# Row products of an encoder block: moving columns and banks downwards in every second set of eight pieces, high parts at eight starts

## The chip, the cores and the metric

The kernel runs on one core of a Trainium2 chip. The metric is the device time of one execution in microseconds (us); lower is better. "Before" is the kernel without the change, "after" the one with it.

## The reference

One layer of a streaming encoder on 256 tokens of 2048 features, all in float32: a half-weighted SwiGLU feed-forward, a mixing block, cross-attention to 256 memory tokens, a second feed-forward and a last norm.

```python
x = x + 0.5 * swiglu(rms_norm(x, ffn1_norm), ffn1_w_up, ffn1_w_down)
h = rms_norm(x, mix_norm)
proj = h @ w_in                       # q, f, i, g, x-branch, gelu gate, two branch gates
...                                   # HGRN2 gives y_a, RG-LRU gives y_b
g = sigmoid(gates + b_gate)
merged = g[0] * (y_a @ w_branch_a) + g[1] * (y_b @ w_branch_b)
x = x + merged @ w_out
x = x + cross_attention(rms_norm(x, xattn_norm), rms_norm(mem, mem_norm), wq, wkv, wo)
x = x + 0.5 * swiglu(rms_norm(x, ffn2_norm), ffn2_w_up, ffn2_w_down)
return rms_norm(x, final_norm)
```

## The kernel before, in words

All weight matrices are streamed once from memory, in pieces of 128 partitions x 2048 columns of float32 (1 MB). A piece lands in a tile `raw` (three buffers). ScalarE writes its high part `h` (rounded to the matmul type float32r, line 126), VectorE the low part `l = raw - h` (line 127); each has three buffers of its own. Activations are held the same way, as a high and a low half. A product of two such numbers is three matmuls: high by high, low by high, high by low.

The pieces come in the order of a list, `plan`, and `weights()` prepares each two ahead of its use. A tile is taken from its pool in turn, and the writer of a buffer waits for the matmuls that last read it. Beyond that the order of the work on each engine is that of the program's text.

Between the two feed-forwards there are two ways to multiply. In `product` (lines 246 and 250; `in`, `q`, `k`) slices of the weight piece are the stationary operand and the activations move. In `rows_product` (lines 267, 268 and 270; `v`, `gate`, `ab`, `out`, `mv`, `o`) the activations are stationary, 128 tokens at a time, and the weight piece moves, 512 columns in one matmul. A piece holds four such slices (`j`, four steps of the contraction) for two halves of the tokens (`t`), so it takes 4 x 2 x 3 = 24 matmuls, each with a weight load of its own: 16 that read `h` and 8 that read `l`. Two PSUM banks, one for each half of the tokens, gather two to four pieces, and are then read by VectorE or ScalarE. The numbers of pieces are `v` 8, `gate` 32, `ab` 16, `out` 16, `mv` 16 and `o` 16.

The feed-forwards take their up-projection apart in a scheme with fewer products (lines 465, 466 and 468), with the weights moving in the same shapes; their tiles `h` come from the same pool.

Of the kernel before, what the change touches and what calls it, by code (L numbers as in the profile page):

```python
# [9 lines left out]
F32R = mybir.dt.float32r  # L10
# [3 lines left out]
P = 128  # L14
# [53 lines left out]
def block_kernel(ctx: ExitStack, tc: tile.TileContext, xT, xin, memT, vec, gfin, bgate, lruw, wu1, wd1, win, wv,  # L68
# [4 lines left out]
    def pool(name, bufs, **kw):  # L73
        return ctx.enter_context(tc.tile_pool(name=name, bufs=bufs, **kw))
# [3 lines left out]
    hp = pool("h", 3)  # L78
    lp = pool("l", 3)
# [19 lines left out]
    def bank(name="acc"):  # L99
        return psum.tile([P, 512], F32, name=name, tag="acc")  # L100
# [24 lines left out]
    def split(h, l, raw):  # L125
        done["high"] = act.activation(h, raw, ACT.Copy).ins  # L126
        done["low"] = dve.tensor_tensor(out=l, in0=raw, in1=h.bitcast(F32), op=ALU.subtract).ins  # L127

    def split_tiles():
        return hp.tile([P, 2048], F32R, name="h", tag="h"), lp.tile([P, 2048], F32R, name="l", tag="l")  # L130


    plan, ahead = [], []
# [12 lines left out]
    def plan_columns(name, w, which):  # L146
        plan.extend(((name, i), w[i], "plain") for i in which)

    def plan_rows(name, w, g):
        plan.extend(((name, g, kq), w[g, kq], "plain") for kq in range(w.shape[1]))  # L150

    plan_ffn("ffn1", wu1, wd1)
    for hf in range(2):
        for base in (8, 0):
            plan_columns("in", win, range(base + hf * 4, base + hf * 4 + 4))
        plan_rows("v", wv, hf)
        plan_columns("in", win, range(16 + hf * 4, 20 + hf * 4))
# [3 lines left out]
    for name, w, n in (("gate", wg, 8), ("ab", wab, 8), ("out", wout, 4)):  # L161
        for g in range(n):
            plan_rows(name, w, g)
    plan_columns("q", wq, range(KT))
    plan_columns("k", wk, range(KT))
    for name, w in (("mv", wvm), ("o", wo)):
        for g in range(4):
            plan_rows(name, w, g)
# [6 lines left out]
    def weights(*key):  # L175
        while plan and len(ahead) < 2:
            i = next(planned)
            k, src, kind = plan.pop(0)
            if i == 0:
                in_turn.enter_context(tc.manual_schedule(engines={sp.engine, act.engine, dve.engine}))  # L180
            if i < len(head):
                head[i]()
            if plan and plan[0][2] == "added":
                begun.append(begin_added(plan[0][1]))
            ahead.append((k, prepare(src, kind, 4 if i < 4 else 1)))
            if i in rest:
                rest[i]()
            if i == 7:
                in_turn.close()
        k, w = ahead.pop(0)  # L190
        assert k == key, (k, key)
        return w
# [3 lines left out]
    def begin_added(src):  # L196

        raw = rawp.tile([P, 2048], F32, name="raw", tag="raw")
        l = lp.tile([P, 2048], F32R, name="l", tag="l")
        sp.dma_start(raw, src)  # L200
        act.activation(l, raw, ACT.Copy, scale=-1.0)
        nc.gpsimd.dma_start(l, src, accum_op=ALU.add)
        return raw, l

    def prepare(src, kind, cuts=1):

        if kind == "added":
            raw, l = begun.pop(0)
            h = hp.tile([P, 2048], F32R, name="h", tag="h")
            done["high"] = act.activation(h, raw, ACT.Copy).ins  # L210
            return h, l
        raw = rawp.tile([P, 2048], F32, name="raw", tag="raw")
        n = 2048 // cuts
        if kind == "plain":
            h, l = split_tiles()
            for a in range(0, 2048, n):
                sp.dma_start(raw[:, a:a + n], src[:, a:a + n])
                split(h[:, a:a + n], l[:, a:a + n], raw[:, a:a + n])
            return h, l
        sp.dma_start(raw, src)  # L220
        td = scoped["wide"].tile([P, 2048], F32, name="td", tag="wide")
        two = [v[:, a:a + 1024].rearrange("p (i n) -> p i n", i=2) for v, a in ((td, 0), (raw, 512))]
        dve.tensor_tensor(out=two[0], in0=raw[:, None, :512].broadcast_to([P, 2, 512]), in1=two[1], op=ALU.subtract)  # L223
        dve.tensor_tensor(out=td[:, 1024:1536], in0=raw[:, 1024:1536], in1=td[:, :512], op=ALU.subtract)
        dve.tensor_tensor(out=td[:, 1536:], in0=raw[:, 1536:], in1=td[:, 1024:1536], op=ALU.subtract)
        h, l = split_tiles()
        if kind == "fast":
            split(h[:, 512:], l[:, 512:], raw[:, 512:])
        else:
            act.activation(l[:, 512:], raw[:, 512:], ACT.Copy, scale=-1.0)  # L230
            nc.gpsimd.dma_start(l[:, 512:], src[:, 512:], accum_op=ALU.add)
            done["high"] = act.activation(h[:, 512:], raw[:, 512:], ACT.Copy).ins
        th = hp.tile([P, 2048], F32R, name="h", tag="h")
        tl = scoped["wide"].tile([P, 2048], F32R, name="tl", tag="wide")
        for a in (0, 1024):
            split(th[:, a:a + 1024], tl[:, a:a + 1024], td[:, a:a + 1024])
        return (h, l), (th, tl)
# [21 lines left out]
        low(range(KT - 4 if was_late else 0, KT))  # L259
        return acc  # L260

    def rows_product(accs, xs, w, k0, first, last):

        terms = [(xs[k0 + j], t, j) for j in range(4) for t in range(2)]
        h, l = ([v[:, j * 512:(j + 1) * 512] for j in range(4)] for v in w)
        for x, t, j in terms:
            pe.matmul(accs[t], x[:, t * P:][:, :P], h[j], start=first and j == 0, stop=False)  # L267
            pe.matmul(accs[t], x[:, T + t * P:][:, :P], h[j], start=False, stop=False)  # L268
        for x, t, j in terms:
            done["product"] = pe.matmul(accs[t], x[:, t * P:][:, :P], l[j], start=False, stop=last and j == 3).ins  # L270
# [210 lines left out]
    def ffn(name, pairs, sq, then, begin=(), sums=()):  # L481
# [37 lines left out]

        for at, e in enumerate(order):  # L520
            w = weights(name, *e)
            kind = e[0]
            following = order[at + 1][0] if at + 1 < len(order) else None
# [101 lines left out]
    w = [par[:, 32 + i * 8:40 + i * 8] for i in range(8)]  # L625
# [52 lines left out]
    xs = xs2.tiles  # L678
# [15 lines left out]
    v = [scoped["extra"].tile([P, 1024], F32, name=f"v{t}", tag="extra") for t in range(2)]  # L694
# [3 lines left out]
    def proj(i):  # L698
        acc = product(xs, weights("in", i), late2)
        if not rs:  # L700
            rs["t"] = sq2.rstd_tokens()
            rs["f"] = by_feature(rs["t"])
        return acc
# [25 lines left out]
    vacc = {}  # L729

    def unit_v(g, kq):
        if kq == 0:
            vacc[g] = [bank(), bank()]
        rows_product(vacc[g], xs, weights("v", g, kq), 4 * kq, kq == 0, kq == 3)
        if kq == 3:
            for t in range(2):
                act.activation(v[t][:, g * 512:(g + 1) * 512], vacc[g][t], ACT.Copy, scale=rs["t"][:, t:t + 1])
# [3 lines left out]
    def unit_gate(g, kq):  # L741

        if kq == 0:
            vacc["gate", g] = [bank(), bank()]
            if g % 2 == 0:
                vacc["bias"] = slot(name="bgate")
                sp.dma_start(vacc["bias"], bgate[:, g * 512:(g + 2) * 512])
        accs = vacc["gate", g]
        rows_product(accs, xs, weights("gate", g, kq), 4 * kq, kq == 0, kq == 3)
        if kq == 3:  # L750
            o = gates[g] = slot(name="gate")
            for t in range(2):
                dve.scalar_tensor_tensor(out=o[:, t * 512:(t + 1) * 512], in0=accs[t], scalar=rs["t"][:, t:t + 1],
                                         in1=vacc["bias"][:, g % 2 * 512:][:, :512], op0=ALU.mult, op1=ALU.add)
            act.activation(o, o, ACT.Sigmoid)
# [154 lines left out]
    for hf in range(2):  # L910
        units += [lambda i=i: unit_f(i) for i in range(hf * 4, hf * 4 + 4)]
        units += [lambda i=i: unit_silu(Q, 0, i) for i in range(hf * 4, hf * 4 + 4)]
        units += [lambda hf=hf, kq=kq: unit_v(hf, kq) for kq in range(4)]
        units += [lambda i=i: unit_silu(G, 16, i) for i in range(hf * 4, hf * 4 + 4)]
        units += [lambda hf=hf: side.append(hgrn(hf)) or True]
# [41 lines left out]
    accs = []  # L957
    for g in range(8):
        accs.append([bank(), bank()])
        for kq in range(2):  # L960
            rows_product(accs[-1], ys.tiles[8 * (g % 2):], weights("ab", g, kq), 4 * kq, kq == 0, kq == 1)
            flush(late)
        if g % 2:
            merge(g // 2, accs)
            accs = []
# [7 lines left out]
    for c in range(4):  # L973
        accs = [bank(), bank()]
# [66 lines left out]
    for g in range(4):  # L1041
        accs = [bank(), bank()]
# [31 lines left out]
    for c in range(4):  # L1074
        accs = [bank(), bank()]
# [127 lines left out]
```

## Time and profile before

| | before |
|---|---|
| median of 3 runs | 2439.36 us (2439.16 to 2440.45) |
| the profiled execution | 2439.93 us |
| its span, first to last instruction | 2438.2 us |
| mean granted TensorE clock | 0.999 |
| TensorE matmul, weight load, busy | 2422.7 us, 2026.4 us |
| VectorE, ScalarE, GpSimd, busy | 1876.3 us, 1479.7 us, 66.5 us |
| read from memory | 537.08 MB, 221 GB/s over the span |

In the profile PE is TensorE with its matmuls and PEld its weight loads, which overlap them; DVE is VectorE, ACT ScalarE, POOL GpSimd and SP the engine that issues most of the DMAs. L267 is line 267 of the kernel. A group's row names the tile written and the tiles read, the count, the busy time, the mean time of one, and the idle time of the engine just before them with what ended it. The chain of waits goes back from the last instruction to what released it; its pieces in order of time give the start, the time and the work. The stretches (windows) give each engine's busy time and, in brackets, its instructions.

### The profile page before, as it was taken

The page shows a single profiled execution, that of the slowest core. Times are in us where ns is not written, and L with a number is a line of the kernel's source. Part 1 is how long each engine was busy: PE and PEld are TensorE (multiplying, and loading weights), DVE is VectorE, ACT ScalarE, POOL GpSimd, SP SyncE. Part 2 cuts the span into 40 slices and gives each one's busy share as a digit, 9 for nine tenths or more (in the row PEclk, how much of TensorE's full clock was granted, in tenths as well). Part 3 has the DMA queues.
Part 4 walks back from the last instruction along what each step waited for, and adds up shares of the span by engine and source line. Part 5 has one row for each costly group of instructions (what it writes and reads, how often), then busy time and mean ns, then how long its engine had stood idle before and what let it go on. Part 6 is the DMA issues. An engine that isn't in the chain of part 4 may idle for free.

```text
span 2438.2 us, 30368 instructions
## 1 busy us (share of the span) xinstructions
PE 2422.7 (99%) x12208; PEld 2026.4 (83%) x12208; DVE 1876.3 (77%) x2051; ACT 1479.7 (61%) x1473; POOL 66.5 (3%) x80
## 2 busy tenths in 40 slices
PE   9999999999999999999999999999999999999998
PEld 8888888888888888888888888888888888888887
DVE  7999999999865767577565676556689899999985
ACT  8567777777654454477435554455555677776774
POOL 0000000000000000000000000000000000000000
PEclk9999999999999999999999999999999999999999
DMA  7578888999855445445555555444555899999984
GB/s 294 193 228 270 272 270 270 272 274 274 255 185 190 174 173 182 173 173 216 195 185 190 210 190 190 172 172 156 190 190 183 265 276 273 266 275 270 271 266 156
DMA packets 81644, 541.14 MB, mean 222 GB/s; under 512 B 9056, under 2 KB 9312, under 8 KB 23136
## 3 DMA queue, kind: packets, MB, share of 16 engines
q1 hardware_dynamic: 69840, 473.06, 53.2%
q0 software_dynamic: 10944, 65.02, 14.2%
q8 instruction: 95, 1.56, 0.3%
q10 hardware_dynamic: 720, 1.13, 0.1%
q14 instruction: 45, 0.37, 0.0%
HBM read 537.08 MB, written 2.10 MB: 221 GB/s over the span
## 4 chain that ended last, share of the span: by engine, by line
PE 89%; DMA 6%; DVE 3%; ACT 1%; issue 1%; ACTq 0%; DVEq 0%; SPq 0%
PE acc L468 16%; PE acc L465 15%; PE acc L466 15%; PE acc L246 11%; PE acc L267 8%; PE acc L268 8%; PE acc L270 8%; PE acc L250 6%; DMA l<-wu 4%; DMA raw<-wu 1%; DVE l L127 1%; PE acc L504 1%; ACT h L126 1%; PE acc L404 1%; ACT l L230 0%
## 5 line engine op out<-in xcount | busy, mean ns | idle before, releaser
L127 DVE TENSOR_TENSOR l<-raw,h 128x2048 fp32r<-128x2048 f32 (+2 forms) x376 | 796.2, 2121 | 330.4 <-ACT h L126 328.5
L126 ACT ACTIVATE h<-raw 128x2048 fp32r<-128x2048 f32 (+2 forms) x376 | 667.3, 1779 | 458.9 <-PE acc L268 207.2
L465 PE MATMUL acc<-h,xh 128*128 128x512 f32 x1254 | 489.1, 391 | 2.1 <-ACT h L126 2.1
L466 PE MATMUL acc<-h,xl 128*128 128x512 f32 x1254 | 487.7, 390 | 0.0
L126 ACT ACTIVATE h<-td 128x1024 fp32r<-128x1024 f32 x252 | 261.9, 1057 | 184.1 <-PE acc L466 96.6
L127 DVE TENSOR_TENSOR tl<-td,h 128x1024 fp32r<-128x1024 f32 x252 | 303.6, 1221 | 70.0 <-ACT h L126 69.2
L267 PE MATMUL acc<-h,ops 128*128 128x512 f32 x832 | 327.3, 393 | 0.0
L268 PE MATMUL acc<-h,ops 128*128 128x512 f32 x832 | 324.7, 390 | 0.0
L465 PEld LDWEIGHTS acc<-h,xh 128*128 128x128 f32 x1254 | 235.6, 188 | 52.4 <-ACT h L126 3.7
L246 PE MATMUL acc<-ops,h 128*128 128x512 f32 x1152 | 278.0, 393 | 0.3
L465 PE MATMUL acc<-h,hidop 128*128 128x512 f32 x704 | 276.1, 392 | 0.0
L466 PEld LDWEIGHTS acc<-h,xl 128*128 128x128 f32 x1254 | 235.6, 188 | 48.5
L466 PE MATMUL acc<-h,hidop 128*128 128x512 f32 x704 | 274.7, 390 | 0.0
L246 PEld LDWEIGHTS acc<-ops,h 128*128 128x128 f32 x1152 | 212.1, 188 | 42.6 <-DVE ops L307 0.9
L270 PE MATMUL acc<-l,ops 128*128 128x512 f32 x832 | 206.2, 390 | 0.0
L468 PE MATMUL acc<-l,xh 128*128 128x512 f32 x750 | 201.0, 391 | 3.2 <-DMA l<-wu 3.1
L468 PE MATMUL acc<-l,hidop 128*128 128x512 f32 x704 | 188.3, 390 | 0.0
L270 PEld LDWEIGHTS acc<-l,ops 128*128 128x128 f32 x832 | 156.3, 188 | 32.3
L267 PEld LDWEIGHTS acc<-h,ops 128*128 128x128 f32 x832 | 156.4, 188 | 32.0
L268 PEld LDWEIGHTS acc<-h,ops 128*128 128x128 f32 x832 | 156.4, 188 | 31.6
L468 PEld LDWEIGHTS acc<-l,xh 128*128 128x128 f32 x750 | 140.1, 188 | 35.8 <-DMA l<-wu 7.4
L223 DVE TENSOR_TENSOR td<-raw 128x1024 f32<-128x1024 f32 x126 | 153.6, 1219 | 3.1 <-DMA raw<-wu 1.3
(222 smaller groups left out, 2583.8 us busy)
## 6 DMA issues: line engine op xcount, KB each, us to landing
raw<-wu SPq DMA_DIRECT2D x172, 1024.0 KB, 6.2
raw<-wd SPq DMA_DIRECT2D x88, 1024.0 KB, 6.1
l<-wu POOLq DMA_DIRECT2D x56, 768.0 KB, 10.0
raw<-win SPq DMA_DIRECT2D x40, 1024.0 KB, 4.8
raw<-wg SPq DMA_DIRECT2D x32, 1024.0 KB, 4.8
l<-wd POOLq DMA_DIRECT2D x16, 1024.0 KB, 10.1
raw<-wab SPq DMA_DIRECT2D x16, 1024.0 KB, 4.8
raw<-wout SPq DMA_DIRECT2D x16, 1024.0 KB, 4.7
```

The source lines that it names most:

```text
L126: done["high"] = act.activation(h, raw, ACT.Copy).ins
L127: done["low"] = dve.tensor_tensor(out=l, in0=raw, in1=h.bitcast(F32), op=ALU.subtract).ins
L223: dve.tensor_tensor(out=two[0], in0=raw[:, None, :512].broadcast_to([P, 2, 512]), in1=two[1], op=ALU.subtract)
L246: pe.matmul(acc, h[:, k * P:(k + 1) * P], xs[k], start=k == 0, stop=False)
L250: done["product"] = pe.matmul(acc[:, :T], l[:, k * P:(k + 1) * P], xs[k][:, :T], start=False, stop=k == KT - 1).ins
L267: pe.matmul(accs[t], x[:, t * P:][:, :P], h[j], start=first and j == 0, stop=False)
L268: pe.matmul(accs[t], x[:, T + t * P:][:, :P], h[j], start=False, stop=False)
L270: done["product"] = pe.matmul(accs[t], x[:, t * P:][:, :P], l[j], start=False, stop=last and j == 3).ins
L404: pe.transpose(accs[m // 2][:, m % 2 * T + t * P:][:, :P], tile[:, t * 512 + m * P:][:, :P], ident)
L465: pe.matmul(acc, ah, bh, start=start, stop=False)
L466: pe.matmul(acc, al, bh, start=False, stop=False)
L468: pe.matmul(acc, ah, bl, start=False, stop=stop)
```

## The change

`h` tiles become 2112 columns wide, of which 2048 are used. For the pieces of `gate`, `ab`, `out`, `mv` and `o`, counted through in the order of the plan, the high part starts at column 0, 4, 8, 16, 24, 32, 40 or 48 of its buffer, in turn. All other pieces start at 0.

`rows_product` counts its uses (those of `v` don't count). In every second set of eight it reads the 512 columns of each slice from the last to the first, in `h` and in `l`, and writes the columns of the two banks in that order too, so each result stands where it stood.

```diff
     def split_tiles():
-        return hp.tile([P, 2048], F32R, name="h", tag="h"), lp.tile([P, 2048], F32R, name="l", tag="l")
+        return hp.tile([P, 2112], F32R, name="h", tag="h")[:, :2048], lp.tile([P, 2048], F32R, name="l", tag="l")
...
+    at_columns, numbers = {}, count()
+
     def plan_rows(name, w, g):
-        plan.extend(((name, g, kq), w[g, kq], "plain") for kq in range(w.shape[1]))
+        for kq in range(w.shape[1]):
+            plan.append(((name, g, kq), w[g, kq], "plain"))
+            if name != "v":
+                i = next(numbers)
+                at_columns[name, g, kq] = (0, 4, 8, 16, 24, 32, 40, 48)[i % 8]
...
-            ahead.append((k, prepare(src, kind, 4 if i < 4 else 1)))
+            ahead.append((k, prepare(src, kind, 4 if i < 4 else 1, at_columns.get(k, 0))))
...
-    def prepare(src, kind, cuts=1):
+    def prepare(src, kind, cuts=1, at=0):
...
-            h, l = split_tiles()
+            h, l = hp.tile([P, 2112], F32R, name="h", tag="h")[:, at:at + 2048], lp.tile([P, 2048], F32R, name="l", tag="l")
...
-    def rows_product(accs, xs, w, k0, first, last):
-
+    used = count()
+
+    def rows_product(accs, xs, w, k0, first, last, turns=True):
+
+        if turns and next(used) // 8 % 2:
+            w = [v.rearrange("p (j n) -> p j n", j=4)[:, :, ::-1] for v in w]
+            accs = [a[:, ::-1] for a in accs]
+            h, l = ([v[:, j] for j in range(4)] for v in w)
+        else:
+            h, l = ([v[:, j * 512:(j + 1) * 512] for j in range(4)] for v in w)
         terms = [(xs[k0 + j], t, j) for j in range(4) for t in range(2)]
-        h, l = ([v[:, j * 512:(j + 1) * 512] for j in range(4)] for v in w)
         for x, t, j in terms:
...
-        rows_product(vacc[g], xs, weights("v", g, kq), 4 * kq, kq == 0, kq == 3)
+        rows_product(vacc[g], xs, weights("v", g, kq), 4 * kq, kq == 0, kq == 3, False)
```

The other places that take an `h` tile take the first 2048 of the 2112 columns.

More of the change, by code (lines that the diff above doesn't have):

```diff
@@ L203, in begin_added @@
         return raw, l
-    def prepare(src, kind, cuts=1):
+    def prepare(src, kind, cuts=1, at=0):
         if kind == "added":
             raw, l = begun.pop(0)
-            h = hp.tile([P, 2048], F32R, name="h", tag="h")
+            h = hp.tile([P, 2112], F32R, name="h", tag="h")[:, :2048]
             done["high"] = act.activation(h, raw, ACT.Copy).ins
@@ L232, in prepare @@
             done["high"] = act.activation(h[:, 512:], raw[:, 512:], ACT.Copy).ins
-        th = hp.tile([P, 2048], F32R, name="h", tag="h")
+        th = hp.tile([P, 2112], F32R, name="h", tag="h")[:, :2048]
         tl = scoped["wide"].tile([P, 2048], F32R, name="tl", tag="wide")
```

## The prediction, made before the change was run

> **What bounds the kernel now.** I read the page first, for the engine that sets the span.
>
> ```profile
> span 2438.2 us, 30368 instructions
> PE 2422.7 (99%) x12208; PEld 2026.4 (83%) x12208; DVE 1876.3 (77%) x2051; ACT 1479.7 (61%) x1473; POOL 66.5 (3%) x80
> ...
> PEclk9999999999999999999999999999999999999999
> ...
> PE 89%; DMA 6%; DVE 3%; ACT 1%; issue 1%; ACTq 0%; DVEq 0%; SPq 0%
> ```
>
> TensorE is busy for 99% of the span at full granted clock, and 89% of the chain that ended last is its own. The change touches the row products (lines 267, 268 and 270), so the next views are the chain of waits, the stretches, the groups and the waits inside 1120 to 1197 us, a stretch made of row products.
>
> ```profile
> by line: PE acc L267 33.8%; PE acc L268 33.5%; PE acc L270 32.3%; PE acc L883 0.7%
> ...
> core 0: us, PE busy (x) PEld busy (x) DVE busy (x) ACT busy (x) POOL busy (x), PEclk, DMA share, GB/s
> 1120.00:1197.00 77.00, 77.00 (x342) 63.80 (x341) 50.51 (x46) 43.87 (x42) 0.00 (x0) 1.00 0.58 205
> ...
> L127 DVE TENSOR_TENSOR l<-raw,h 128x2048 fp32r<-128x2048 f32 x15 | 34.2, 2286 | 13.5 <-ACT h L126 13.5
> L126 ACT ACTIVATE h<-raw 128x2048 fp32r<-128x2048 f32 x16 | 30.5, 1915 | 32.2 <-PE acc L268 27.4 <-DVE ops L304 3.3 <-DMA raw<-wg 1.2
> ```
>
> There TensorE never idles, VectorE works 50.5 of 77 us, ScalarE 43.9, the DMA engines 0.58. ScalarE waits for TensorE (27.4 of its 32.2 idle us) to give back a buffer of `h`. So a change in the pace of a matmul goes into the time in full, and nothing on the other engines does.
>
> Next, the pace, from the timeline of TensorE: the first matmuls of two pieces.
>
> ```profile
> 1120.74 0.39 PE L267 MATMUL acc<-h,ops 128*128 128x512 f32 x1
> ...
> 1196.90 0.39 PE L267 MATMUL acc<-h,ops 128*128 128x512 f32 x1
> ```
>
> Between the two starts lie 14 pieces of 24 matmuls: 76.16 / 336 = 226.7 ns from one matmul to the next. (The 0.39 us in a row is a matmul's length to its modelled end, and overlaps the next one; the pace is what costs time.) How much of it is columns shows beside the low matmuls of the column products, which have 256 columns (chain of waits):
>
> ```profile
> 716.93 1.91 PE acc L250 x16
> ```
>
> They stand 119.4 ns apart, so 256 further columns cost 226.7 - 119.4 = 107.3 ns: an estimate of 0.42 ns a column, 214.6 ns for 512, and 12.1 ns between two matmuls.
>
> **Part by part: the direction.** Pieces are counted over `gate` (32), `ab` (16), `out` (16), `mv` (16) and `o` (16), 96 in all; `v` is left out. Sets 1, 3, 5 and so on of 8 go downwards: 48 pieces, each with all 24 of its matmuls (the low parts `l` and the banks are turned as well), so 48 x 24 = 1152 matmuls. Count, shapes, weights, order and waits stay. The whole price is what one downward matmul costs against 226.7 ns, with TensorE the bound.
>
> Every matmul in the trace reads its moving columns upwards and writes its bank upwards, so that price has to be bounded. The nearest row with a slower stream is that of the plain fp32 matmuls, which the array takes at half the column rate (chain of waits, 14 matmuls in a row):
>
> ```profile
> 1069.99 3.02 PE acc L883 x14
> ```
>
> That is 215.7 ns for 256 columns, 431.4 ns for 512. The array thus has two paces here: a column per tick for the rounded type, a column per two ticks for plain fp32. If a downward stream can't be fetched or accumulated in pairs, it falls from the first to the second: 431.4 - 226.7 = 204.7 ns, times 1152 = 235.8 us. With the 12.1 ns between matmuls kept whole the price is 2 x 214.6 + 12.1 - 226.7 = 214.6 ns, or 247.2 us: the upper bound. The lower bound is a gain: if turning the stream took away all but what plain fp32 leaves between two matmuls (215.7 - 214.6 = 1.1 ns), each would stand 11.0 ns closer, 12.7 us in all. I take 235.8 us. The bounds are far apart, and the row nearest to a stream that no longer gets its columns at full rate is that of line 883.
>
> The trace does not speak for the gain: the 12.1 ns don't come from a weight load that fights with the moving columns, as the timeline of matmuls and of weight loads shows around a break.
>
> ```profile
> 1120.29 0.62 PE L270 MATMUL acc<-l,ops 128*128 128x512 f32 x2
> ...
> 843.55 0.61 PE L270 MATMUL acc<-l,ops 128*128 128x512 f32 x2
> ...
> 843.10 0.64 PEld L270 LDWEIGHTS acc<-l,ops 128*128 128x128 f32 x3
> 844.09 0.64 PEld L780 LDWEIGHTS acc<-silu,k 128*32 128x32 f32 x64 [0.35 <-issue]
> ```
>
> The loads pause from 843.74 to 844.09, so the second matmul of the pair from 843.55 runs with no load beside it, and the pair is as long (0.61 us) as one in full traffic (0.62 us).
>
> Two rules of the Trainium skill speak to the direction. *PSUM — Partial Sum Buffer*, section "Specifications (TRN2)", gives 8-byte lines and says that any non-contiguous pattern slows matmuls significantly; *Advanced Engine Details and Errata*, section "PSUM Cachelines", adds that every two consecutive elements should be contiguous. Read strictly, a falling pair is not, and the rule speaks against the change; it states no factor, and no run here shows it yet. The same page's "SBUF Cachelines" asks only for two hits on a 16-byte line, which falling fp32 columns still give; by that rule alone the sum would be nothing.
>
> **The distances.** In all 96 pieces the high part starts 0 to 48 columns into its buffer. 96 x 16 = 1536 matmuls read it. In the trace every slice starts a multiple of 128 columns into its tile, so a start 4 columns in is not shown; buffers and slices that stand far apart have one pace:
>
> ```profile
> L466 PE MATMUL acc<-h,xl 128*128 128x512 f32 x1254 | 487.7, 390 | 0.0
> ...
> L268 PE MATMUL acc<-h,ops 128*128 128x512 f32 x832 | 324.7, 390 | 0.0
> ...
> L270 PE MATMUL acc<-l,ops 128*128 128x512 f32 x832 | 206.2, 390 | 0.0
> ```
>
> I take 0. The most that a disturbed phase costs here is seen in the column products after a break, in the chain of waits:
>
> ```profile
> 718.85 3.65 PE acc L246 x16
> ...
> 802.53 3.85 PE acc L246 x16
> ```
>
> That is 0.20 us over 16, 12.5 ns a matmul, so 0 to 19.2 us for 1536; no gain, since 226.7 ns holds for each distance that occurs. ScalarE's writing of `h` (1915 ns) and VectorE's reading of it (2286 ns) at the new starts lie under a piece of 24 x 226.7 = 5.44 us; uncovered, only what they grew by would count.
>
> **The rest.** `h` grows by 64 columns in three buffers, which moves all tiles behind it by 768 bytes a partition: nothing, by the same rows. No wait is added and no DMA moved. Pieces that last twice as long ask less of the queues: the weights, which land in 4.8 us, have 10.4 us.
>
> ```profile
> raw<-wg SPq DMA_DIRECT2D x32, 1024.0 KB, 4.8
> ```
>
> **Sum.** The profiled execution took 2439.93 us, span 2438.2. 2439.93 + 235.8 = 2675.7; the median of the three runs, 2439.36, stands 0.57 lower: 2675 us.
>
> **Rivals.** *Downwards costs nothing* (the other side): fetch and accumulation go by lines, and a falling stream meets each line as often as a rising one, or the two reversals are folded into one rising access before the chip sees them, so that nothing is changed. For it: no idle time, wait or count changes. It decides if the pace in the downward sets stays at 226.7 ns; the time is 2439 us. Between the two I choose by the array's having a half pace that it falls to for one kind of operand already.
>
> *A small price per matmul*: a falling stream needs a longer start, of the size of the disturbed phase, 12.5 ns x 1152 = 14.4 us: 2454 us. For it: paces between 227 and 240 ns do occur. Against it: they settle within a piece.
>
> *Half pace at some distances only*: at the four starts that aren't a multiple of 16 columns (4, 8, 24, 40), in downward pieces, high parts: 24 x 16 = 384 matmuls x 204.7 ns = 78.6 us: 2518 us. Nothing in the trace for or against it.
>
> *Faster*: the downward stream loses the gap, -12.7 us: 2427 us. Against it is the pair without a weight load. The weights would not hold it back: a piece of 24 x 215.7 ns is 5.18 us, above the 4.8 us of a landing. *TensorE: Matmul & The Clock Gate*, section "Back-to-back issue gap", gives N/2.4 + 2.5 ns for isolated matmuls; the 226.7 ns here lie above that, and by that rule there is such a gap to win, 12.6 us; nothing there ties it to a direction.
>
> **Numbers.** Half pace in all downward matmuls 0.38, no cost 0.24, small price 0.16, some distances only 0.10, faster 0.12. The time is that of the likeliest, 2675 us; its own range is 2655 to 2695 (the two prices, 235.8 and 247.2 us, and up to 10 us of phases at the joints and starts). The whole range has to take in no cost, which lies on the other side: 2434 to 2695 us, from no cost less 0.2% up to the upper bound (2687) and some phases; outside it are the gain, 0.12, and a price beyond half pace. 0.2%, 4.9 us, is about what a measurement of this kernel can tell from no change. Slower by more: 0.38 + 0.16 + 0.10 = 0.64; within it 0.24; faster by more 0.12.
>
> **What the changed profile would show.** Half pace: row products in two kinds of pieces, 5.4 us and 10.4 us long, eight by eight, with TensorE busy throughout, the clock still full, and ScalarE's wait for lines 268 and 270 longer. No cost: all pieces 5.44 us. Small price: downward pieces of 5.7 us. Some distances: pieces of two lengths inside one downward set. Faster: 5.18 us. I am wrong if the downward matmuls start within 235 ns of each other, or if the feed-forwards, whose code is the same, change their pace because the tiles moved.

## The result and the profile after

The kernel with the change takes 2451.91 us (median of 4 runs, 2450.37 to 2452.95), the one before 2439.26 us (4 runs): 1.0049 times as long, 95% interval 1.0037 to 1.0061, 12.65 us more. The profiled execution took 2451.54 us, its span is 2449.8 us.

The page of the changed kernel, first the engines and the chain, then the groups of matmuls. Lines 478 and 479 are the former 465 and 466 of the feed-forwards; 280, 281 and 283 the former 267, 268 and 270 of the row products.

```profile
span 2449.8 us, 30370 instructions
...
PE 2433.6 (99%) x12208; PEld 2024.8 (83%) x12208; DVE 1876.5 (77%) x2051; ACT 1480.5 (60%) x1473; POOL 66.6 (3%) x80
...
PE 92%; DMA 5%; ACT 1%; DVE 1%; issue 0%; ACTq 0%; SPq 0%; DVEq 0%
...
L478 PE MATMUL acc<-h,xh 128*128 128x512 f32 x1254 | 488.4, 390 | 1.8 <-ACT h L126 1.8
L479 PE MATMUL acc<-h,xl 128*128 128x512 f32 x1254 | 487.0, 389 | 0.0
...
L280 PE MATMUL acc<-h,ops 128*128 128x512 f32 x832 | 331.5, 398 | 0.0
L281 PE MATMUL acc<-h,ops 128*128 128x512 f32 x832 | 328.8, 395 | 0.0
```

VectorE, ScalarE and the counts are what they were. The feed-forwards keep their 390 ns, although all tiles behind `h` moved by 768 bytes (three times 256, a shift that by the experiments below would not be felt). Lines 280 and 281 rose to 398 and 395 ns, from 390 for line 268 and, for line 267, from the 393 of this row of before:

```profile
L267 PE MATMUL acc<-h,ops 128*128 128x512 f32 x832 | 327.3, 393 | 0.0
```

So the time is in the row products. There TensorE still never idles, as the stretch of 77 us shows:

```profile
core 0: us, PE busy (x) PEld busy (x) DVE busy (x) ACT busy (x) POOL busy (x), PEclk, DMA share, GB/s
1120.00:1197.00 77.00, 77.00 (x333) 62.23 (x332) 50.37 (x46) 43.83 (x43) 0.00 (x0) 1.00 0.56 198
```

It holds 333 matmuls where there were 342: each takes longer. How much longer shows in the chain of waits, whose pieces hold the eight low matmuls of a weight piece (start, us, work):

```profile
1148.71 1.86 PE acc L283 x8
1159.92 1.87 PE acc L283 x8
...
1182.29 1.81 PE acc L283 x8
1187.81 1.84 PE acc L283 x8
```

The first two are downward pieces: 1.87 / 8 = 0.234 us from start to start. The third is an upward piece with its high part at 0: 1.81 / 8 = 0.226 us, the pace of before. The fourth is upward as well, but its high part began 4 columns in, and its low part (at 0) had not yet settled. For the sixteen high matmuls, the timeline gives the first of them and the first low one, in two upward pieces, starts 8 and 16:

```profile
1096.69 0.40 PE L280 MATMUL acc<-h,ops 128*128 128x512 f32 x1
...
1100.43 0.40 PE L283 MATMUL acc<-l,ops 128*128 128x512 f32 x1
...
1195.07 0.40 PE L280 MATMUL acc<-h,ops 128*128 128x512 f32 x1
...
1198.75 0.39 PE L283 MATMUL acc<-l,ops 128*128 128x512 f32 x1
```

3.74 / 16 = 233.8 ns and 3.68 / 16 = 230.0 ns. The steps from start to start in the trace over all pieces (matmuls 5 to 16, so the high parts alone, and six pieces in each place):

```
start of the high part     0      4      8     16     24     32     40     48
upwards, ns            226.9  231.7  233.3  229.0  233.8  233.0  234.3  233.3
downwards, ns          233.3  233.3  233.3  233.3  233.3  235.0  233.3  233.3
```

There are two prices. Downward pieces stand on the mean of all their 24 steps 6.5 ns a matmul above before, 1152 x 6.5 = 7.5 us, and their start makes no difference but at 32 (235.0 ns). Upward pieces stand 4.1 ns above it on the same mean, which takes in the low parts, 1152 x 4.1 = 4.7 us, and those at start 0 not at all. Together that is 12.2 of the 12.65 us.

### The profile page after: what moved, and what is told of

Its sections match the earlier page's. It is cut to its first block, busy times and chain, and to the rows that moved or that the text cites. A ratio compares the mean times of both kernels' runs of the same rounds, so it can differ in the third digit from the quotient of the medians.

```text
span 2449.8 us, 30370 instructions
## 1 busy us (share of the span) xinstructions
PE 2433.6 (99%) x12208; PEld 2024.8 (83%) x12208; DVE 1876.5 (77%) x2051; ACT 1480.5 (60%) x1473; POOL 66.6 (3%) x80
## 4 chain that ended last, share of the span: by engine, by line
PE 92%; DMA 5%; ACT 1%; DVE 1%; issue 0%; ACTq 0%; SPq 0%; DVEq 0%
PE acc L481 16%; PE acc L478 16%; PE acc L479 16%; PE acc L252 11%; PE acc L280 8%; PE acc L281 8%; PE acc L283 8%; PE acc L256 6%; DMA l<-wu 5%; PE acc L517 1%; PE acc L417 1%; ACT l L236 1%; DMA raw<-wu 0%; ACT h L126 0%; PE acc L793 0%; PE acc L1030 0%
## 5 line engine op out<-in xcount | busy, mean ns | idle before, releaser
L280 PE MATMUL acc<-h,ops 128*128 128x512 f32 x832 | 331.5, 398 | 0.0
L281 PE MATMUL acc<-h,ops 128*128 128x512 f32 x832 | 328.8, 395 | 0.0
```

## The experiments

The steps below are means from the start of one matmul to the start of the next, with the few steps that hold a pause left out. Where no interval stands beside a total time, the kernel ran once and the time is rough; the steps are what is read.

**One part at a time.** The first kernel has the turns alone:

```diff
-                at_columns[name, g, kq] = (0, 4, 8, 16, 24, 32, 40, 48)[i % 8]
+                at_columns[name, g, kq] = 0
```

> The change without its starts: every high part begins at column 0 of its buffer; the 48 downward pieces stay. In the profile of the changed kernel the 48 downward pieces stand at 233.6 ns a matmul whatever their start, against 227.1 before. Theory A (the direction has a price of its own, about 6.5 ns a matmul, and the starts have another one that only upward pieces pay): 1152 x 6.5 = +7.5 us, 2446.8 us, ratio 1.003; upward pieces back at 226.7 ns. Rival B (the upward pieces slow down because the downward ones before them leave the array out of phase): 2451.9 us, with upward pieces at 229 to 234 ns here too.

It took 2446.75 us, ratio 1.0029 (1.0018 to 1.0041). Chain of waits, an upward and a downward piece:

```profile
1094.92 1.81 PE acc L283 x8
...
1159.23 1.87 PE acc L283 x8
```

All upward pieces are back at 226.7 ns, all downward ones stand at 233.3. The second kernel has the starts alone:

```diff
-        if turns and next(used) // 8 % 2:
+        if turns and next(used) < 0:
```

> The change without its turns: the eight starts in all 96 pieces, every piece upwards. Theory A: the upward pieces of the changed kernel stand 4.1 ns a matmul above before on the mean of the eight starts, so 2304 x 4.1 = +9.4 us, 2448.7 us, ratio 1.004, with 226.7 ns at start 0, about 230 at 16 and 231 to 233 at the others. Rival B (starts cost only beside downward pieces): 2439.3 us, 226.7 ns everywhere.

It took 2449.45 us, ratio 1.0040 (1.0026 to 1.0054). The timeline has a piece at start 8, and one at 0 that stands where a downward piece stood:

```profile
1188.55 0.40 PE L280 MATMUL acc<-h,ops 128*128 128x512 f32 x1
...
1192.29 0.40 PE L283 MATMUL acc<-l,ops 128*128 128x512 f32 x1
...
1222.84 0.39 PE L280 MATMUL acc<-h,ops 128*128 128x512 f32 x1
...
1226.47 0.62 PE L283 MATMUL acc<-l,ops 128*128 128x512 f32 x2
```

233.8 and 226.9 ns: all eight starts come out as in the upward pieces of the change, in both kinds of sets. So theory A holds, and rival B falls. The parts add up: turns 7.45 us, starts in half the pieces 10.15 / 2 = 5.1 us, 12.5 of 12.65.

**Reading or accumulating.** `way` counts the sets of eight modulo 4:

```diff
+        if way in (1, 3):
+            h, l = ([v[:, ::-1] for v in part] for part in (h, l))
+        if way in (2, 3):
+            accs = [a[:, ::-1] for a in accs]
```

> All starts 0. The sets of eight take four forms in turn, 24 pieces each: upwards; only the moving columns downwards; only the bank downwards; both. In the second and third form the columns of the result come out in reverse order, a changed computation. Theory Read (the price is that of fetching the moving columns): 226.7, 233.3, 226.7, 233.3 ns a matmul, total +7.5 us. Rival Bank (the price is that of accumulating at falling addresses): 226.7, 226.7, 233.3, 233.3, total +7.5 us. Rival Both ends (a price where reading and writing run against each other): 226.7, more than 226.7, more than 226.7, something else.

It took 2448.31 us beside 2439.3. Chain of waits, in order a piece with only the moving columns downwards, one with only the bank, one with both, one with neither:

```profile
1053.10 1.87 PE acc L283 x8
...
1095.58 1.81 PE acc L283 x8
...
1148.69 1.87 PE acc L283 x8
...
1187.64 1.81 PE acc L283 x8
```

Over all pieces: 233.4, 226.9, 233.4 and 227.4 ns. The bank's direction costs nothing; the whole price goes with the direction in which the moving columns are read.

**Where the weights lie.** Here the stationary operand is shifted, the high part is not:

```diff
-            pe.matmul(accs[t], x[:, t * P:][:, :P], h[j], start=first and j == 0, stop=False)
+            pe.matmul(accs[t], x[:, t * P + d:][:, :P], h[j], start=first and j == 0, stop=False)
```

> High parts at start 0; the 96 pieces upwards and downwards by sets as in the change; instead of the moving columns it is the stationary operand that begins 0, 4, 8, 16, 24, 32, 40 or 48 columns later, in turn by pieces (so it multiplies shifted tokens, a changed computation). Theory Distance (what counts is how far the moving columns and the weights that are loaded meanwhile lie from each other within 256 bytes): upward pieces at 229 to 234 ns at seven of the eight starts, 226.7 at 0; downward ones stay at 233.3. Rival Moving alone (what counts is where the moving columns begin, whatever is loaded beside them): 226.7 ns in all upward pieces, 233.3 in all downward ones, total +7.5 us.

It took 2451.07 us beside 2439.3. Chain of waits: upward pieces with the weights at 0, 4, 16 and 48, and a downward one:

```profile
1182.38 1.81 PE acc L283 x8
1187.82 1.82 PE acc L283 x8
...
1198.97 1.87 PE acc L283 x8
...
1222.17 1.83 PE acc L283 x8
1227.73 1.87 PE acc L283 x8
```

The moving columns did not move, and the pace changed. The steps in the high parts, with those of the kernel that has the starts alone at the opposite start (64 columns less the shift, 256 bytes being 64 columns):

```
weights at              0      4      8     16     24     32     40     48
upwards, ns         226.8  228.9  233.2  233.3  234.1  232.5  233.4  228.9
moving columns at       0      -      -     48     40     32     24     16
upwards, ns         227.1      -      -  233.3  234.4  232.8  233.9  229.0
```

All six pairs that can be compared agree within 0.5 ns: what counts is the distance, not where the moving columns begin. Moving alone falls. Downward pieces stay at 233.2 to 233.4 ns at all eight shifts of the weights, as they did at seven of the eight starts of the moving columns. So the downward price is not the distance in another form, although a downward stream begins 511 columns further on, 4 bytes short of a multiple of 256. The next kernel shifts both by the same number of columns:

```diff
+        n = next(used) if turns else 0
+        d = (0, 4, 8, 16, 24, 32, 40, 48)[n % 8] if turns else 0
...
-            pe.matmul(accs[t], x[:, t * P:][:, :P], h[j], start=first and j == 0, stop=False)
+            pe.matmul(accs[t], x[:, t * P + d:][:, :P], h[j], start=first and j == 0, stop=False)
```

> All pieces upwards. The high part begins 0 to 48 columns into its buffer as in the change, and the stationary operand of the matmuls that read it begins as many columns later (it multiplies shifted tokens, a changed computation); the low part and its weights stay at 0. Theory Distance: 226.7 ns a matmul inside the high parts at every start, with disturbances only at the joints to the low parts, where the two differ. Rival Moving alone or Each by itself: 229 to 234 ns inside the high parts as with the starts alone.

It took 2443.68 us beside 2439.51. In the timeline of a piece at start 8, six steps late in its high part:

```profile
1189.04 0.39 PE L277 MATMUL acc<-h,ops 128*128 128x512 f32 x1
...
1190.40 0.39 PE L277 MATMUL acc<-h,ops 128*128 128x512 f32 x1
```

1.36 / 6 = 226.7 ns. At the end of the high part the pace is 226.6 or 226.7 at every start but 4, after a disturbance of up to ten matmuls from the joint. At 4 it stays at 230.1 to the end of the high part. So distance is shown for shifts of 8 columns and more, and fails for the shift of 4, which is half of the smallest of those. The scan of other starts says the same:

```diff
-                at_columns[name, g, kq] = (0, 4, 8, 16, 24, 32, 40, 48)[i % 8]
+                at_columns[name, g, kq] = (2, 12, 20, 28, 36, 44, 52, 60)[i % 8]
```

> The change with eight other starts: 2, 12, 20, 28, 36, 44, 52 and 60. Theory Distance: with the weights shifted, 16 and 48 columns gave 233.3 and 228.9 ns where the moving columns at 48 and 16 gave 233.3 and 229.0, so moving columns at 60 should be as weights at 4, 229 ns; the others 229 to 235 upwards, 2 somewhere from 227 to 232 (half a start of 4), none below 226.7; downward pieces 233.3, at most 236.5. Rival (there is a start that lets the two streams pass each other): one of them below 226.7 ns, down to the 215.7 that the plain fp32 matmuls' gap would leave.

It took 2452.43 us beside 2439.51. Upwards 233.8, 232.8, 231.1, 231.1, 233.3, 232.6, 234.4 and 234.4 ns. Start 60 was expected at 229 and came at 234.4: a miss, again with a shift of 4. Start 2 was expected at 227 to 232 and came at 233.8. Downward pieces stand at 233.3 ns, but at 235.5 with start 2. No start is below 226.7, so the rival falls.

**Whose load.** Only every second high matmul gets shifted weights:

```diff
-            pe.matmul(accs[t], x[:, T + t * P:][:, :P], h[j], start=False, stop=False)
+            pe.matmul(accs[t], x[:, T + t * P - t * (d > 0) * 64 + d:][:, :P], h[j], start=False, stop=False)
```

> All pieces upwards, high parts at 0; only the stationary operand of every second high matmul (line 278, the low half of the activations) begins 0, 8, 16, 24, 32, 40, 48 or 56 columns later (a changed computation). Theory Meanwhile (what counts is the load that runs while a matmul streams, that is the next one's): the step from a matmul of line 277 to that of line 278 grows, the step from 278 to the next 277 stays near 226.7. Rival Own (what counts is a matmul's own weights): the step from 278 to the next 277 grows, the other stays. The low parts stay at 226.7 either way.

This is inconclusive. Both steps grow, at 8 columns for instance from 227 to 232 (277 to 278) and from 227 to 236 (278 to 277). The steps run in cycles of two to eight matmuls, so a disturbed step shifts the next one, and the two can't be told apart. The kernel took 2446.41 us beside 2439.51.

**How long the load is.** `c` is 128, 96 or 64 by sets:

```diff
-            pe.matmul(accs[t], x[:, T + t * P:][:, :P], h[j], start=False, stop=False)
+            pe.matmul(accs[t][:c], x[:, T + t * P:][:, :c], h[j], start=False, stop=False)
```

> Starts 0. The sets of eight take six forms in turn, 16 pieces each: upwards with 128, 96 and 64 stationary columns, then downwards with 128, 96 and 64 (the first matmul of a bank and the last keep 128; tokens beyond the columns taken lose terms, so part of the computation is left out). Theory Load (everything above the 512 columns' own time is made by the load's reads): the 12 to 13 ns above 213.3 to 214.6 shrink with the columns: upwards 226.7, 223.3, 220.0 ns a matmul; downwards 233.3, 228.3, 223.3. Rival Fixed (the 12 ns are a fixed step between matmuls, and the load adds only the 6.7 ns of the downward pieces): upwards 226.7 three times, downwards 233.3, 231.7, 230.0.

It took 2449.29 us beside 2439.51. Chain of waits: 96 and 64 columns upwards, then 128, 96 and 64 downwards:

```profile
1056.53 1.84 PE acc L285 x8
...
1098.76 1.83 PE acc L285 x8
...
1152.34 1.87 PE acc L285 x8
...
1197.14 1.87 PE acc L285 x8
...
1243.69 1.87 PE acc L285 x8
```

Upwards 227.2, 230.2 and 230.2 ns, downwards 233.4 three times. Both theories fall. A load of half the columns, 135 ns in its rows where the full one has 188, costs no less; upwards it costs 3 ns more.

**How long the stream is.** First 512 against 256 moving columns:

```diff
+        c = 256 if way > 1 else 512
+        part = lambda a, c: a[:, :c][:, ::-1] if way % 2 else a[:, :c]
```

> Starts 0. The sets of eight take four forms in turn, 24 pieces each: upwards with 512 moving columns, downwards with 512, upwards with 256, downwards with 256 (the first and the last matmul of a bank keep 512; the other columns lose terms, so part of the computation is left out). Upwards with 256 should stand about 120 ns apart, as the 256-column matmuls of the column products do. Theory Step (the price of a downward stream is paid once a matmul): 226.7, 233.3, 120, 126.7 ns. Rival Stream (it is paid with every column, 6.7 ns for 512): 226.7, 233.3, 120, 123.3 ns.

Pieces of 256 columns are so short that many wait for their weights (2345.5 us in all); in those that don't, upward matmuls stand 120.0 ns apart and downward ones 118.3. Both theories fall: at 256 columns downwards is the faster way. The kernel before with its column products turned says it again:

```diff
-                pe.matmul(acc, h[:, k * P:(k + 1) * P], xs[k], start=k == 0, stop=False)
+                pe.matmul(acc[:, ::-1], h[:, k * P:(k + 1) * P], xs[k][:, ::-1], start=k == 0, stop=False)
```

> The kernel before, with the column products turned instead of the row products: in all 72 pieces of in, q and k the activations move downwards and the bank with them, 1152 matmuls of 512 columns and 1152 of 256, while the weight pieces are stationary. Theory (the price belongs to any downward moving operand): 512 columns at 233.3 ns against 226.7, and 256 at about 126.7 (price once a matmul) or 123.3 (price by columns) against 119.4: total +15.4 or +12 us. Rival (it belongs to the buffers of the row products, whose weights lie in the operand slots): no change, 2439 us.

It took 2445.2 us beside 2440.12. Chain of waits, the sixteen high matmuls (512 columns) and the sixteen low ones (256):

```profile
1372.16 3.73 PE acc L246 x16
1375.90 1.89 PE acc L250 x16
```

3.73 stands against 3.65 before and 1.89 against 1.91: the long ones lose, the short ones gain, with other buffers as moving and as stationary operand. In the settled part of a piece the steps are 233.3 and 118.3 ns, against 226.8 and 120.0 before. So the theory is right for 512 columns and wrong for 256, and the rival falls. The gain at 256 columns alone, in the kernel before:

```diff
-                done["product"] = pe.matmul(acc[:, :T], l[:, k * P:(k + 1) * P], xs[k][:, :T], start=False,
+                done["product"] = pe.matmul(acc[:, :T][:, ::-1], l[:, k * P:(k + 1) * P], xs[k][:, :T][:, ::-1], start=False,
```

> The kernel before with one turn alone: the low parts of the column products (line 250, 1152 matmuls of 256 columns) read and write downwards; everything else upwards. In the run with all column products downwards these stood 118.3 ns apart where upward ones stand at 120.0. Theory: 1152 x 1.7 = 1.9 us less, less a joint of up to 10 ns at each of the 72 pieces (0.7 us): about 2438 us, ratio 0.9993 or so, which five rounds may not tell from 1; the pace of line 250 in the profile tells. Rival Mixed (upward and downward matmuls beside each other cost as in the kernel by turns): slower in the first matmuls of each piece by more than the gain, 2440 us or above.

2437.04 us against 2439.66, ratio 0.9991 (0.9982 to 1.0000). Chain of waits:

```profile
1371.90 3.63 PE acc L246 x16
1375.53 1.89 PE acc L250 x16
```

A column piece takes 3.63 + 1.89 = 5.52 us instead of 3.65 + 1.91 = 5.56; in the trace lines 246 and 250 lose 2.2 us in all. Only 1.3 of that is in line 250, which was turned; 0.9 is in line 246, whose first two steps behind a downward low part are shorter (227 and 230 ns, 233 and 235 before). So the joint helped, where the theory took a loss, and Mixed falls. The interval by itself just reaches 1. It is the fastest version here that does the whole computation. The last kernel of this kind takes other lengths:

```diff
+        c = (480, 448, 384, 320, 192, 128)[way // 2] if turns else 512
```

> Starts 0. The twelve sets of eight go upwards and downwards in turn, with 480, 448, 384, 320, 192 and 128 moving columns, one upward and one downward set each (the first and the last matmul of a bank keep 512; the rest of the columns loses terms, part of the computation is left out). Theory Even (upwards a matmul takes its columns at 0.417 ns and 13.3 ns more, at every length that the load doesn't bound): 213.3, 200.0, 173.3, 146.7 ns, then the load's own pace of about 107 to 110 ns at 192 and 128. Theory Meeting (the price depends on where the two reads stand to each other when one ends, so downwards it changes sign with the length): downward ones above the upward ones at some lengths, as at 512 (+6.7 ns), and below at others, as at 256 (-1.7 ns). Rival Monotone (the price grows with the length): downwards minus upwards falls steadily from +6.7 at 512 to -1.7 at 256.

With 512 and 256 from the kernels above, ns from start to start:

```
moving columns      512    480    448    384    320    256
upwards           226.7  216.9  204.6  173.3  146.7  120.0
downwards         233.3  220.0  206.9  177.8  146.7  118.3
difference         +6.7   +3.1   +2.3   +4.5    0.0   -1.7
```

At 192 and at 128 columns the settled step is 111.7 ns both ways. The columns no longer set it; that the weight load does is argued, not shown. Stretches that wait for weights, at a lower granted clock (0.76 from 1600 to 1640 us), came in there, so those lengths say nothing of the direction. Even falls (480 and 448 upwards have 16.9 and 17.9 ns above 0.417 ns a column, the others 13.3). Monotone falls too, as 384 has a larger difference than 448. That the difference changes sign with the length is what Meeting said, but no run places the meeting.

**Neighbours.** Upward and downward matmuls by turns:

```diff
+            down = (0, n % 2, n // 2 % 2, n // 4 % 2)[way]
+            return (acc[:, ::-1], moving[:, ::-1]) if down else (acc, moving)
```

> Starts 0, the whole computation. The sets of eight take four forms in turn, 24 pieces each: all upwards; every second matmul downwards; two up and two down; four up and four down (moving columns and bank turned together). Theory Own price (a downward matmul costs 6.7 ns, whatever stands beside it): 226.7 ns on the mean of the first form, 230.0 of each of the others, total +3.8 us. Rival Joint (what costs is that a stream begins far from where the last one ended: an upward one right after a downward one on the same slice begins where it ended): every second matmul downwards comes out at 226.7 or below, and the forms differ from each other.

It took 2452.76 us beside 2440.12. All upwards 227.4 ns; by single turns 234.5, by twos 234.5, by fours 232.5. Both theories fall. A mixture costs as much as or more than going downwards throughout (233.4): the step depends on the matmuls beside it.

## Why the prediction was wrong

**The bound held.** The prediction said that TensorE's pace goes into the time in full and that nothing is added on other engines. The row products keep it busy for 77.00 of 77 us, and the longer steps account for 12.2 of the 12.65 us measured.

**The step that failed is the size of a downward matmul.** It was taken from line 883, the plain fp32 matmuls at half the column rate: 204.7 ns a matmul, 235.8 us. Measured are 6.5 ns and, with the turns alone, 7.45 us, about one thirtieth. The reason given, that a falling stream can't be fetched or accumulated in pairs, is refuted at both ends: a falling bank costs nothing, and a falling fetch nearly keeps the column rate (from 256 to 512 columns it takes 233.3 - 118.3 = 115.0 ns more, 0.45 ns a column, where upward ones take 0.42 and the row of line 883 has 0.84). Nothing tied that row to direction. It was also misread as one matmul at a slower stream:

```profile
L883 PE MATMUL acc<-xc,lw x32: 377/379/484, 1069.8 to 1114.1; 128*128 128x256 f32 x32
```

Line 883 makes 16 matmuls (2 x 4, for each of two halves), and the trace has 32 records, 215.7 ns apart. So each plain fp32 matmul leaves two records and takes 431.4 ns for its 256 columns. The row shows a matmul that is done in two goes; whether the array streams more slowly within one of them, no run shows.

The sign of being wrong that the prediction named came: downward matmuls start 233.4 ns apart, within 235. The time of 2451.91 us does lie in the range of 2434 to 2695, but only because the range was drawn wide enough to take in no cost. That is no support for the half pace.

The rule of the Trainium skill that was weighed there, *Advanced Engine Details and Errata*, section "PSUM Cachelines", is not borne out here in the strict reading, by which a falling pair is not contiguous: 226.9 ns with the bank downwards against 227.4 without. Its section "SBUF Cachelines" agrees as far as it goes: the column rate was nearly kept, 0.45 against 0.42 ns.

**The starts** were costed at 0, with 0 to 12.5 ns as bounds. They cost 4.1 ns on the mean of the eight upwards, and downwards only 1.7 ns at start 32. The ground for 0, that buffers far apart have one pace, was true and said nothing: in the kernel before all of them lie a multiple of 256 bytes from the weights.

**The pair without a weight load** was used to say that the load doesn't matter. It compared lengths to a modelled end, and the conclusion was too wide: moving only the weights changes the step by up to 7 ns. Whether the 12 ns that were there before come from the load stays open; they don't shrink with its columns.

**The rivals.** The small price, 2454 us, was the case that came, at 2451.91. It was sized from a disturbed phase in the column products, 12.5 ns on the downward matmuls alone; in its place stand 6.5 ns there and 4.1 ns on the upward ones, which the rival left out. That the two sums are so near, 14.4 and 12.65 us, is luck. That paces between 227 and 240 ns settle within a piece was held against it. Upward steps settle at 226.7 only while both streams lie at a multiple of 256 bytes from each other (and not with both shifted by 4 columns); otherwise they stay higher, as the table of starts shows. No cost falls, as the downward sets stand at 233.3 ns with the starts at 0. Half pace at some distances falls, as downward pieces at 4, 8, 24 and 40 stand at 233.3 as well. The gain of 12.7 us did not come: no start and no direction is below 226.7 ns at 512 columns.

## What to carry to other kernels

Where TensorE is the bound with a weight load before each float32r matmul, compare steps from start to start, not lengths or busy shares: 2 to 3% of pace in the row products, a fifth of the matmuls, left the busy share at 99% and moved the mean length by 1%. Keep the moving columns and the stationary ones a multiple of 256 bytes apart, as they were in the kernel before, and let 512 moving columns go upwards; padding a tile by a few columns, or slicing into it, can cost 3% of every matmul that reads it. An upper bound taken from an operation of another kind is a bound, not a forecast, unless something in the trace ties the two together.

## What the runs showed of the hardware

The step of one matmul with a weight load is not a fixed sum: it runs from 226.7 to 235.5 ns at 512 columns by the distance between the moving columns and the weights within 256 bytes, by the direction, and by the direction of the matmuls beside it. The weight load has a part in it although the rows show it only overlapping (188 ns each). The Trainium skill, page *TensorE: Matmul & The Clock Gate*, section "Step-by-step: what each phase is for", says that loading the next weights takes no read bandwidth from the running matmul; here a shift of the weights alone moves the step from 226.8 to 234.1 ns, so the two are not independent, by whatever way. Reading backwards is 6.7 ns slower at 512 columns, even at 320 and 1.7 ns faster at 256. What joins the distance, the direction and the length into one rule stays open.
